# A planned step kernel on one core: a first-user rule, softmax weights of a third unit through DRAM, masked low parts in the weights' place, and another count for later loads

## The chip, the core and the metric

The kernel runs on one core of a Trainium2 chip. The metric is device time in microseconds (us) from one launch, the median of several runs. The engines are called as in the profile: PE (TensorE, matmuls; PEld is its weight load), DVE (VectorE), ACT (ScalarE), POOL (GpSimd) and SP (SyncE), whose queue issues all DMAs of this kernel. Each engine works through its own list in order; what one needs of another it awaits on a semaphore.

## What is computed

One inference step of a decoder with two layers, for 512 rows of a prompt and 8 samples of one row each, with the same weights. Layer A is a gated recurrence of 16 heads (HGRN2), layer B a sliding-window attention of 32 query heads over 4 key heads, window 128, with a sink logit for each head. Around each layer stand RMS norms, a residual and a gated embedding.

```python
def sink_softmax(s, sinks):
    sink = sinks.astype(jnp.float32).reshape(KV_HEADS, Q_PER_KV)[:, :, None, None]
    sink = jnp.broadcast_to(sink, s.shape[:-1] + (1,))
    pr = jax.nn.softmax(jnp.concatenate([s, sink], axis=-1), axis=-1)
    return pr[..., :-1]
...
        mask = in_band & ((cidx >= WINDOW) | (n > 0))
        s = jnp.einsum('bqhgd,bkhd->bhgqk', qn.astype(jnp.float32), kn.astype(jnp.float32)) * ATTN_SCALE
        s = jnp.where(mask, s, -jnp.inf)
        pr = sink_softmax(s, sinks)
        return jnp.einsum('bhgqk,bkhd->bqhgd', pr, vn.astype(jnp.float32))
...
        h = h + rmsnorm(mix, post_norm_g[l])
        h = h + (p[l] @ w_pe[l]) * jax.nn.sigmoid(h @ w_pg[l])
```

## The kernel before

Activations lie transposed, 128 features on the partitions by 520 columns. Every float32 operand of a matmul is split in a high part, rounded to the PE's narrower float32r by a cast on ACT, and a low part, the remainder, mostly from a subtraction on DVE (in the names: wh and wl of weights wr, x or og as pairs). A weight load of 512 KB brings a tile wr; pj are PSUM banks of projections, ph those of everything else.

The program runs through the 16 heads of layer A (their projections, the recurrence, and in groups the output projection out_a), then the boundary (rest of out_a, embedding, the sum of squares acc over x, its reciprocal root rsr, residual, gates, the norm for keys and values), then layer B, then the same kind of boundary again for the end. Layer B has eight units of four query heads. Function unit_proj projects queries and gates of a unit, block makes the softmax for one of four blocks of 128 queries, and out_b projects outputs in groups; out_b(6) of units 2 and 3 stands behind unit 5's projections, out_b(8) of units 4 and 5 behind unit 7's.

In block, W holds the four heads' logits of one block with the sink beside them, in a buffer of tag b3 (blocks 1 and 2) or b2 (blocks 0 and 3), three buffers each. ACT copies the logits there, takes the exponentials and their sum ad, DVE or POOL multiplies by its reciprocal. Then the weights have to be turned so that keys lie on the partitions. For the units in TURN_W that is done by turn_weights: two transposes of 32 x 32 blocks on DVE, one store to a DRAM tile tw and four loads back into W's buffer, then a cast on ACT for the high part and a subtraction for the low one. For all others PE transposes W against an identity (ident) into a PSUM bank, four at a time, and ACT and DVE make both parts from there. In blocks 1 to 3 both parts are also multiplied by a mask (tmask) into ys[0] and ys[1]; up to unit 6 two DMAs then move halves of the masked low part into the empty halves of ys[0].

The order of all instructions is found when the kernel is built, by class Plan. Method enter records an operation with the operations that it depends on: those that wrote or read overlapping regions, and, for every buffered tile that it touches, the tile's maker, the first operation that touched it. Method issue then places one operation after another on the engine that could start it first, by planned costs and delays, and the instructions are held to that order; so all have one line in the profile, L192. Of the operations that an engine could start, choose prefers those whose inputs don't come fresh from a DMA, then by level (MAIN, SIDE, FIRST), then by number. An operation is considered only when its number is less than WINDOW, or for DMAs LOADS, ahead of the lowest one not yet placed (low). An operation entered through either may go to DVE or POOL; POOL takes it where DVE has enough else to do. The point where layer B begins is second.

Of the kernel before, what the change touches and what calls it, by code (L numbers as in the profile page):

```python
# [9 lines left out]
F32 = mybir.dt.float32  # L10
F32R = mybir.dt.float32r
# [10 lines left out]
SEQ = 512  # L22
# [17 lines left out]
PIECE = 4 * P  # L40
SPLITS = 4
TURN_K, TURN_O = range(0, 15), range(1, 15)
TURN_W = (4, 5)
WARM = 17
BEHIND = 4

# [3 lines left out]
MAIN, SIDE, FIRST = 0, 1, 2  # L50
# [44 lines left out]
class Plan:  # L95
# [91 lines left out]
    def enter(self, on, name, a, k):  # L187
        outs = [k["accum_out"]] if "accum_out" in k else []
        outs.append(a[0])
        ins = [x for x in (*a, *k.values()) if isinstance(x, bass.AP)]  # L190
        calls = [getattr(getattr(self.nc, e), name) for e in on]
        op = Op(len(self.ops), self.level, on, [lambda c=c: c(*a, **k) for c in calls],  # L192
                [self.price(e, name, ins, a, k) for e in on], on[0] == "sync")
        if any(x.tensor.name.startswith("tw") for x in ins[1:]):
            op.late = LATE
        self.ops.append(op)
        for x in ins:
            t = x.tensor.name
            r = self.region(x)
            op.deps.update(o for q, o in self.writes.get(t, ()) if self.meet(q, r))  # L200
            self.reads.setdefault(t, []).append((r, op))
            kept = t in self.homes or x.space != bass.MemoryType.DRAM
            if kept and t not in self.left:
                tag, bufs = self.homes.get(t, (t, 1))
                if tag not in self.slots:
                    self.slots[tag] = Slots(tag, bufs)
                self.slots[tag].order.append(t)
                op.news.append((tag, t))
                self.maker[t] = op
            elif kept:  # L210
                op.deps.add(self.maker[t])
            if t not in op.tiles and kept:
                op.tiles.add(t)
                self.left[t] = self.left.get(t, 0) + 1
        for x in outs:
            t = x.tensor.name
            r = self.region(x)
            if on[0] == "tensor":
                r = 0, P, r[2] // 512 * 512, -(-r[3] // 512) * 512
            for book in (self.writes, self.reads):  # L220
                old = book.get(t, [])
                op.deps.update(o for q, o in old if o is not op and self.meet(q, r))
                book[t] = [(q, o) for q, o in old if o is op or not self.within(q, r)]
            self.writes.setdefault(t, []).append((r, op))
        op.deps.discard(op)
        op.load = op.dma and not op.deps
        for d in op.deps:
            d.users.append(op)
        op.open = len(op.deps)
        return op  # L230


    def issue(self):
# [3 lines left out]
        given, pipe, lanes, low, port, slow = set(), 0.0, [0.0] * 8, 0, 0.0, 0.0  # L237
        best = dict.fromkeys(clock)
        stale = set(clock)

        def after(d, e):

            if d.dma:
                return d.end + 0.1
            return d.end + (SAME if d.engine == e else LAT)[d.engine]

        def ready(op, e):
            return max((after(d, e) for d in op.deps), default=0.0)

        def place(op):  # L250
            at = 0.0
# [9 lines left out]
        def choose(e):  # L261
            able = []
            for op, r in wait[e]:
                p = place(op) if op.n < low + (LOADS if op.dma else WINDOW) else None
                if p is not None:
                    held = port if op.cost[op.on.index(e)][1] else 0.0
                    if op.dma and op.load and clock[e] > CALM and pipe > BACKLOG + op.cost[0][0]:
                        held = pipe - BACKLOG - op.cost[0][0]
                    able.append((max(r, p, clock[e], held), op, max(r, p)))
            if not able:  # L270
                return None
            t = min(x[0] for x in able)
            rank = RANK.get(e, OTHER)
            able = [x for x in able if x[0] <= t]
            safe = SAFE if t > CALM and low < self.second else 0.0
            fresh = lambda op: any(d.dma and d.end + safe > t for d in op.deps)
            able.sort(
                key=lambda x: (
                    e == "tensor" and x[2] + HAND > t or e in SHY and fresh(x[1]), rank[x[1].level], x[1].n
                )  # L280
            )
            if e == "gpsimd":
                for x in able:
                    op = x[1]
                    if len(op.on) > 1:

                        free = [
                            o.cost[0][0]
                            for o, r in wait["vector"]
                            if r <= t and not o.cost[0][1] and place(o) is not None  # L290
                        ]
                        if max(clock["vector"] - t, 0.0) * (port <= t) + sum(free) < op.cost[1][0]:
                            continue
                    return x
                return None
            return able[0]
# [6 lines left out]
        while todo:  # L303
# [11 lines left out]
            if op.n == low:  # L315
                while low < len(self.ops) and self.ops[low].engine:
                    low += 1
                stale.update(clock)
            cost, held = op.cost[n]
            if op.dma:  # L320
                t = max(t, lanes[0])
# [69 lines left out]
def in_turn(tiles):  # L391

    for t in tiles[1::2]:
        t.apart = True
    return tiles


def bank_of(ps, h):
# [56 lines left out]
class Step:  # L455
# [871 lines left out]
    def block(self, u, st, n, osb):  # L1327
# [52 lines left out]
                nc.tensor.matmul(po, base[0][:, kvh % 2], w, start=x == 0, stop=x == 1)  # L1380
        else:

            ys = [self.g_(F32R, SEQ) for x in range(2)]
            by = lambda x: x.rearrange("p (i h t) -> p i h t", h=4, t=run)
            mask = spot(self.tmask, 0, (run, P // run), (0, 4), (1, run))
            for x, y in zip((hi, lo), ys):
                nc.either.tensor_tensor(by(y), by(x.bitcast(F32)), mask, op=ALU.mult)
            y, z = (x.bitcast(F32) for x in ys)
            if u < 7:
                nc.sync.dma_start(y[HD:, : 4 * HD], z[:HD, : 4 * HD])  # L1390
                nc.sync.dma_start(y[:HD, 4 * HD :], z[HD:, 4 * HD :])
# [158 lines left out]
    def run(self):  # L1550
# [66 lines left out]
        def done_a(h):  # L1617
# [6 lines left out]

            return f

        for h in range(HEADS):
            tiles += self.proj_a(h, xg if h == 0 else xn, sts[h], done_a(h), R0 if h == 0 else None)
            if h + 1 in groups:
                tiles += out_a(h + 1)  # L1630
        tiles += out_a(17)
        end = out_a(18) + self.embed(0, pe[0], range(E0, KC), kept[0]) + self.embed(1, pe[1], range(E1))

# [47 lines left out]
        for u in range(8):  # L1681
            def done(u=u):
                self.beside(lambda: self.unit_attn(u, us[u]))
                if u % 4 == 3:
                    self.beside(lambda: self.sample_out(u // 4, us[u - 3 : u + 1]), FIRST)

            mine = self.unit_proj(u, qx, us[u], done)
            if u == 7:

                tiles[-2:-2] = mine[:2]  # L1690
                mine = mine[2:]
            tiles += mine
            if u + 1 in ogroups:
                tiles += out_b(u + 1)
        tiles += out_b(9)
        end1 = out_b(10) + self.embed(1, pe[1], range(E1, KC), kept[1])

# [143 lines left out]
```

## Time and profile before

| | |
|---|---|
| Runs, median (lowest to highest) | 1068.3 us (1067.65 to 1070.68, three runs) |
| The profiled execution's own time | 1068.61 us |
| Its span, first to last instruction | 1066.8 us |
| Granted TensorE clock | 0.999 |
| Busy: PE, PEld, DVE, ACT, POOL | 1057.2, 1051.2, 904.7, 681.8, 114.0 us |
| DMA | 178.99 MB, 161 GB/s of HBM over the span |

Busy time is the union of an engine's instructions; matmuls overlap, so a record of 0.28 us doesn't mean that a matmul costs PE as much. The chain of waits follows the work that ended last back in time; the view of waits tells for how long an engine stood still and which engine's result released it.

### The profile page before, as it was taken

Reading aid. Unit: us, or ns where it says so; the run is one execution under the profiler, and the core shown is the slowest. Engines: PE = TensorE matmul, PEld = TensorE weight load, DVE = VectorE, ACT = ScalarE, POOL = GpSimd, SP = SyncE. Lnnn points to the kernel's source line nnn. Section 1 sums busy time; section 2 is a strip of 40 time slices with the busy share of each in tenths; the row PEclk is TensorE's granted clock in tenths of the full one; section 3 lists DMA queues with packets and bytes.
Section 4 is the critical chain, followed back from the end, with each engine's and each line's share of the span. In section 5 each row is a group of like instructions: output and inputs, shape, how many; then the busy total and the mean of one; then the engine's idle time right before and its main releaser. Section 6 shows DMA issues by size and latency. Waiting matters only on the chain.

```text
span 1066.8 us, 23981 instructions
## 1 busy us (share of the span) xinstructions
PE 1057.2 (99%) x8828; PEld 1051.2 (99%) x8828; DVE 904.7 (85%) x1963; ACT 681.8 (64%) x1829; POOL 114.0 (11%) x198
## 2 busy tenths in 40 slices
PE   9999999999999999999999999999999999999998
PEld 8999999999999999999999999999999999999998
DVE  8899788875787958788889999699999998999894
ACT  7877676655767637776636565477667664675542
POOL 1111121101111112111111000000100000002000
PEclk9999999999999999999999999999999999999999
DMA  9556586665646646576663454544433545423432
GB/s 314 183 190 183 143 247 195 191 195 156 213 155 206 193 130 224 177 210 191 190 223 142 159 190 142 170 121 136 124 101 115 164 155 186 154 82 124 156 100 81
DMA packets 147069, 178.99 MB, mean 168 GB/s; under 512 B 76932, under 2 KB 99660, under 8 KB 146952
## 3 DMA queue, kind: packets, MB, share of 16 engines
q1 hardware_dynamic: 146952, 177.46, 52.7%
q8 instruction: 70, 1.15, 0.4%
q14 instruction: 47, 0.39, 0.1%
HBM read 137.04 MB, written 34.86 MB: 161 GB/s over the span
## 4 chain that ended last, share of the span: by engine, by line
PE 91%; ACT 4%; DVE 3%; issue 1%; DMA 0%; POOL 0%; DVEq 0%; POOLq 0%
PE pj L192 71%; PE ph L192 21%; ACT g L192 1%; ACT wh L192 1%; DVE wl L192 1%; DVE x L192 0%; DMA wr<-in_w_pg 0%; ACT tmp L192 0%; ACT sb L192 0%; ACT b L192 0%; DVE acc L192 0%; ACT og L192 0%; DVE xr L192 0%; DVE tmp L192 0%; DVE g L192 0%
## 5 line engine op out<-in xcount | busy, mean ns | idle before, releaser
L192 PE MATMUL pj<-xs,wh 128*128 128x260 f32 (+2 forms) x3264 | 554.7, 285 | 1.6 <-ACT xs L192 1.3
L192 PEld LDWEIGHTS pj<-xs,wh 128*128 128x128 f32 x3264 | 457.7, 189 | 3.2 <-ACT xs L192 2.3
L192 PE MATMUL pj<-xs,wl 128*128 128x260 f32 (+2 forms) x1632 | 340.5, 285 | 0.0
L192 PEld LDWEIGHTS pj<-xs,wl 128*128 128x128 f32 x1632 | 255.1, 188 | 0.2
L192 ACT CAST wh<-wr 128x512 fp32r<-128x512 f32 x287 | 176.2, 619 | 111.1 <-PE pj L192 100.5
L192 DVE TENSOR_TENSOR wl<-wr,wh 128x512 fp32r<-128x512 f32 x275 | 187.6, 685 | 48.6 <-ACT wh L192 47.4
L192 PE MATMUL pj<-og,wh 128*128 128x260 f32 x1056 | 182.4, 285 | 0.3 <-ACT og L192 0.3
L192 PEld LDWEIGHTS pj<-og,wh 128*128 128x128 f32 x1056 | 149.5, 188 | 0.9 <-ACT og L192 0.5
L192 PE MATMUL pj<-og,wl 128*128 128x260 f32 x512 | 106.3, 284 | 0.1
L192 PEld LDWEIGHTS pj<-og,wl 128*128 128x128 f32 x512 | 79.9, 188 | 0.3 <-DVE wl L192 0.3
L192 ACT ACTIVATE sb<-sb,g 128x128 f32<-128x128 f32 x128 | 64.7, 556 | 2.4 <-DVE sb L192 2.4
L192 ACT ACTIVATE sb<-sb,nv 128x128 f32<-128x128 f32 x128 | 63.1, 555 | 0.3
L192 ACT COPY b<-ph 128x256 f32<-128x256 f32 (+1 forms) x80 | 27.8, 350 | 47.0 <-PE ph L192 46.5
L192 ACT ACTIVATE b<-b,an 128x129 f32<-128x129 f32 x128 | 50.6, 398 | 4.5 <-DVE an L192 4.4
L192 ACT ACTIVATE tmp<-pj 128x520 f32<-128x520 f32 (+2 forms) x48 | 24.5, 527 | 43.3 <-PE pj L192 43.2
L192 PE MATMUL ph<-xs,b 128*128 128x256 f32 (+1 forms) x360 | 50.5, 283 | 0.0
L192 DVE COPY_PREDICATED xr<-lmask,ph 128x256 f32<-128x256 int32 x96 | 46.8, 487 | 3.8 <-PE ph L192 3.4
L192 PE MATMUL ph<-xr,b 128*128 128x128 f32 x320 | 49.0, 275 | 0.3 <-ACT b L192 0.3
L192 DVE TENSOR_TENSOR x<-x,pj 128x520 f32<-128x520 f32 (+2 forms) x64 | 39.5, 621 | 10.8 <-PE pj L192 10.2
L192 DVE TENSOR_TENSOR g<-g,b 128x256 f32<-128x256 f32 x96 | 40.5, 422 | 9.3 <-ACT b L192 6.1
L192 DVE TENSOR_TENSOR xr<-xr,b 128x256 f32<-128x256 f32 x96 | 41.0, 427 | 8.6 <-PE ph L192 6.4
L192 PEld LDWEIGHTS ph<-xs,b 128*128 128x128 f32 x360 | 46.3, 188 | 0.1
(222 smaller groups left out, 1737.8 us busy)
## 6 DMA issues: line engine op xcount, KB each, us to landing
wr<-in_w_in_a SPq DMA_DIRECT2D x64, 512.0 KB, 4.5
sb<-sd SPq DMA_DIRECT2D x32, 512.0 KB, 4.5
wr<-in_w_in_b SPq DMA_DIRECT2D x32, 512.0 KB, 4.0
td<-tmp SPq DMA_DIRECT2D x45, 256.0 KB, 3.2
xr<-td SPq DMA_DIRECT2D x180, 64.0 KB, 3.2
sb<-in_state SPq DMA_DIRECT2D x16, 512.0 KB, 5.4
out_st_s<-sb SPq DMA_DIRECT2D x16, 512.0 KB, 3.0
wr<-in_w_out_a SPq DMA_DIRECT2D x16, 512.0 KB, 4.8
```

Of the source, the lines that this page charges most:

```text
L192: op = Op(len(self.ops), self.level, on, [lambda c=c: c(*a, **k) for c in calls], [self.price(e, name, ins, a, k) for e in on], on[0] == " ...
```

## The change

Five edits stand in the diff. TURN_W takes in unit 3. The masked low part ys[1] is written into W's own buffer (home) instead of a g buffer, up to unit 6. A dependency that exists only because another operation was the first to touch the tile becomes soft: it still orders the two, but it counts for nothing in the planned time, nor as fresh from a DMA. From second on, a load of level MAIN is considered by its distance from the next matmul of level MAIN not yet placed, instead of from low. A function weave, which could put the tiles of an output projection between those of the next head or unit, is added; its lists WEAVE_A and WEAVE_B are empty, and then it returns its tiles as they were.

```diff
-TURN_W = (4, 5)
+TURN_W = (3, 4, 5)
+WEAVE_A, WEAVE_B = (), ()
...
+        makers = set()
...
             elif kept:
-                op.deps.add(self.maker[t])
+                makers.add(self.maker[t])
...
         op.deps.discard(op)
+        op.soft = makers - op.deps - {op}
+        op.deps |= op.soft
         op.load = op.dma and not op.deps
...
+        main, front = [op for op in self.ops if op.level == MAIN and "tensor" in op.on], 0
...
-            return max((after(d, e) for d in op.deps), default=0.0)
+            return max((after(d, e) for d in op.deps if d not in op.soft), default=0.0)
...
-                p = place(op) if op.n < low + (LOADS if op.dma else WINDOW) else None
+                first = main[front].n if op.load and op.level == MAIN and front < len(main) and low >= self.second else low
+                p = place(op) if op.n < first + (LOADS if op.dma else WINDOW) else None
...
-            fresh = lambda op: any(d.dma and d.end + safe > t for d in op.deps)
+            fresh = lambda op: any(d.dma and d.end + safe > t for d in op.deps if d not in op.soft)
...
+            while front < len(main) and main[front].engine:
+                front += 1
+                stale.add("sync")
...
+def weave(mine, out):
+
+    n = -(-len(out) // len(mine))
+    return [x for k, t in enumerate(mine) for x in (t, *out[k * n : (k + 1) * n])]
...
-            ys = [self.g_(F32R, SEQ) for x in range(2)]
+            ys = [self.g_(F32R, SEQ), spot(home, 0, (1, SEQ)) if u < 7 else self.g_(F32R, SEQ)]
...
-            y, z = (x.bitcast(F32) for x in ys)
+            y, z = (x.bitcast(F32) if x.dtype == F32R else x for x in ys)
```

What this moves is seen in the order of the instructions. Over the program PE has 16 transposes fewer and DVE eight block transposes more; of the low parts of weights (wl<-wr,wh) POOL has 21 instead of 12, of the multiplications by the reciprocal sum (b<-b,ad) 6 instead of none, and of the mask products 3 instead of 8. Three places in detail.

In unit 3, PE before turns a block's weights (b_2043_2137) between products of the next unit's queries (pj_2217), its logits (ph_2163) and out_b (pj_2280):

```order
L192 MATMUL ph_2163<-xr_1788,g_2094 128x256
L192 MATMUL ph_2163<-xr_1792,g_2094 128x256
L192 MATMUL ph_2144<-ident,b_2043_2137 128x2x64 x4
L192 MATMUL pj_2217<-xs_1725,wh_2209 128x260
L192 MATMUL pj_2280<-og_1890,wh_2212 128x260 x2
```

Now DVE does it, for unit 3's first block (b_2024_2118) in this stretch of its list (g_2187 is a low part of the next unit's queries):

```order
L193 TENSOR_TENSOR wl_2194<-wr_2192,wh_2193 128x512
L193 STREAM_TRANSPOSE tmp_2125<-b_2024_2118 128x2x4x32
L193 SCALAR_TENSOR_TENSOR g_2187<-tmp_2184,g_2186 128x512
L193 STREAM_TRANSPOSE tmp_2125<-b_2024_2118 128x2x4x32
L193 RECIPROCAL ad_2133<-ad_2133 128x4
```

and SP has the stores and loads of unit 3's weights among the loads of weights (wr) and the exchange of queries' halves (qd):

```order
L193 DMA tw_2126<-tmp_2125 128x512
L193 DMA wr_2274<-in_w_out_b 128x1024
L193 DMA g_2186<-qd_2188 64x512
L193 DMA g_2187<-qd_2188 64x512
L193 DMA b_2024_2118<-tw_2126 32x4x128 x2
L193 DMA qd_2199<-g_2197 64x512
L193 DMA b_2024_2118<-tw_2126 32x4x128
L193 DMA qd_2199<-g_2198 64x512
L193 DMA b_2024_2118<-tw_2126 32x4x128
L193 DMA tw_2137<-tmp_2136 128x512
```

So a block's weights now pass from DVE through SP's queue to ACT, and PE's list holds only the products with values.

At the boundary between the layers, PE sums the squares of the first half (ph_1528<-ones,acc_1506) before at this place, behind all of pj_1565, three matmuls of the embedding (pj_1595) and two of ph_1571:

```order
L192 MATMUL pj_1565<-xs_1450,wh_1500 128x264 x2
L192 MATMUL pj_1595<-g_1591,wh_1561 128x260 x2
L192 MATMUL pj_1595<-g_1591,wl_1562 128x260
L192 MATMUL ph_1571<-xs_1379,wh_1504 128x264
L192 MATMUL ph_1571<-xs_1379,wl_1505 128x264
L192 MATMUL ph_1528<-ones,acc_1506 128x1 x2
L192 MATMUL ph_1571<-xs_1380,wh_1504 128x264
```

and now ahead of pj_1565, behind ph_1559:

```order
L193 MATMUL ph_1558<-xs_1450,wh_1495 128x264
L193 MATMUL ph_1559<-xs_1450,wh_1495 128x264
L193 MATMUL ph_1528<-ones,acc_1506 128x1 x2
L193 MATMUL pj_1565<-xs_1379,wh_1500 128x264 x2
L193 MATMUL pj_1565<-xs_1379,wl_1501 128x264 x2
```

It has moved ahead by 17 matmuls. On DVE the additions that it waits for ended before with these rows (wl_1568, a low part of weights, stood on POOL):

```order
L192 TENSOR_TENSOR x_724<-x_724,pj_1556 128x264
L192 TENSOR_TENSOR acc_1506<-acc_1506,tmp_1517 128x256
L192 TENSOR_TENSOR wl_1562<-wr_1560,wh_1561 128x512
L192 TENSOR_TENSOR acc_1506<-acc_1506,tmp_1518 128x256
L192 TENSOR_TENSOR acc_1506<-acc_1506,tmp_1557 128x264
```

and now with these; wl_1568 follows on the same engine, eleven rows behind the last addition (tmp_1518):

```order
L193 TENSOR_TENSOR acc_1506<-acc_1506,tmp_1517 128x256
L193 TENSOR_TENSOR x_719<-x_719,pj_1556 128x264
L193 TENSOR_TENSOR acc_1506<-acc_1506,tmp_1518 128x256
L193 TENSOR_TENSOR x_724<-x_724,pj_1556 128x264
L193 TENSOR_TENSOR wl_1562<-wr_1560,wh_1561 128x512
L193 TENSOR_TENSOR x_728<-x_728,ph_1558 128x264
```

The last addition of the first half (tmp_1518) now stands ahead of x_724 and wl_1562 instead of behind them.

At the start, SP before loads the second part of tmask behind the first weights of layer A:

```order
L192 DMA tmask<-in_tmask 128x64
L192 DMA wr_98<-in_w_pe 128x512
L192 DMA vec<-in_vec 128x88
L192 DMA x_104<-in_xT 128x520
L192 DMA x_105<-in_xT 128x520
L192 DMA x_106<-in_xT 128x520
L192 DMA x_107<-in_xT 128x520
L192 DMA wr_108<-in_w_in_a 128x1024
L192 DMA tmask<-in_tmask 128x64
L192 DMA x_111<-in_xT 128x520
```

and now both parts ahead of them:

```order
L193 DMA tmask<-in_tmask 128x64 x2
L193 DMA wr_98<-in_w_pe 128x512
L193 DMA vec<-in_vec 128x88
L193 DMA x_104<-in_xT 128x520
L193 DMA x_105<-in_xT 128x520
```

One load has moved ahead of seven.

More of the change, by code (lines that the diff above doesn't have):

```diff
@@ L1625, in done_a @@
             return f
+        out = []
         for h in range(HEADS):
-            tiles += self.proj_a(h, xg if h == 0 else xn, sts[h], done_a(h), R0 if h == 0 else None)
-            if h + 1 in groups:
-                tiles += out_a(h + 1)
+            tiles += weave(self.proj_a(h, xg if h == 0 else xn, sts[h], done_a(h), R0 if h == 0 else None), out)
+            out = out_a(h + 1) if h + 1 in groups else []
+            if h + 1 not in WEAVE_A:
+                tiles += out
+                out = []
         tiles += out_a(17)
@@ L1691, in run @@
                 mine = mine[2:]
-            tiles += mine
-            if u + 1 in ogroups:
-                tiles += out_b(u + 1)
+            tiles += weave(mine, out)
+            out = out_b(u + 1) if u + 1 in ogroups else []
+            if u + 1 not in WEAVE_B:
+                tiles += out
+                out = []
         tiles += out_b(9)
```

## The prediction

> **What bounds the kernel now.** I read the page's first and fourth parts, then the windows of 100 us, the chain of waits, and the waits of TensorE by what released it.
>
> ```profile
> span 1066.8 us, 23981 instructions
> ...
> PE 1057.2 (99%) x8828; PEld 1051.2 (99%) x8828; DVE 904.7 (85%) x1963; ACT 681.8 (64%) x1829; POOL 114.0 (11%) x198
> ...
> PE 91%; ACT 4%; DVE 3%; issue 1%; DMA 0%; POOL 0%; DVEq 0%; POOLq 0%
> ```
>
> PE is busy in 99% of the span and carries 91% of the chain that ended last; DVE, the next, is at 85%. The windows (columns: window and its length, then the busy time of PE, PEld, DVE, ACT and POOL) show where this is an average over unlike stages:
>
> ```profile
> 0.00:100.00 100.00, 97.25 (x791) 94.78 (x792) 89.84 (x191) 76.05 (x170) 16.16 (x43) 1.00 0.66 218
> ...
> 700.00:800.00 100.00, 100.00 (x839) 99.65 (x838) 94.82 (x201) 68.56 (x223) 8.29 (x7) 1.00 0.40 122
> 800.00:900.00 100.00, 100.00 (x833) 99.59 (x832) 90.67 (x185) 64.98 (x199) 3.89 (x3) 1.00 0.49 154
> 900.00:1000.00 100.00, 100.00 (x838) 99.58 (x837) 92.50 (x193) 59.86 (x184) 8.34 (x6) 1.00 0.43 143
> ```
>
> From 700 to 1000, where layer B's units run, PE has no gap at all. A busy PE need not be a PE at its pace, so I look for the pace in the chain of waits:
>
> ```profile
> 652.55 33.96 PE pj L192 x283
> ```
>
> 283 matmuls in 33.96 us are 0.120 us each from start to start; that is what a projection matmul costs while nothing holds it up. What PE loses besides is small and has names:
>
> ```profile
> PE pj L192 <- ACT xs L192: 1.3, 2, 0.8
> PE ph L192 <- DVE far L192: 1.1, 1, 1.1
> PE pj L192 <- DVE g L192: 0.9, 2, 0.6
> PE ph L192 <- ACT b L192: 0.5, 2, 0.3
> PE ph L192 <- DVE acc L192: 0.5, 1, 0.5
> PE ph L192 <- POOL rsr L192: 0.4, 1, 0.4
> PE pj L192 <- ACT og L192: 0.3, 1, 0.3
> PE ph L192 <- DVE ad L192: 0.2, 1, 0.2
> ```
>
> That is 5.2 us in all, 1.1 of it the start of the program. So the change can win in two ways only: fewer matmuls, at their pace, or fewer of these waits. And it loses wherever it makes PE wait in a stretch that is full today. No DMA is among the releasers: PE waits for no load.
>
> **The change part by part.**
>
> *Unit 3's weights through DRAM.* Sixteen transposes leave PE (four blocks, four each). What four of them cost stands between the matmuls around them (a block of unit 2; columns: start, time, what, how many):
>
> ```profile
> 788.64 0.40 PE L192 MATMUL pj<-xs,wl 128*128 128x260 f32 x2
> 788.88 0.60 PE L192 MATMUL ph<-ident,b 128*128 128x128 f32 x4
> 789.23 0.73 PE L192 MATMUL pj<-xs,wh 128*128 128x260 f32 x4
> 789.80 0.28 PE L192 MATMUL pj<-xs,wl 128*128 128x260 f32 x1
> ```
>
> From 788.64 to 789.80 are 1.16 us, in which six projection matmuls and four transposes start. Six at 0.12 are 0.72; 0.44 is left for four transposes, 0.11 each. Sixteen: **-1.75 us**, and all of it on the path, since PE is full there. In before the last of unit 3's transposes also wait for the softmax's sum (the 0.2 us of "DVE ad" above); the transposes that wait are gone: **-0.2 us**.
>
> [...]
>
> In their place come eight transposes on DVE and, per block, one store and four loads:
>
> ```profile
> L192 DVE STREAM_TRANSPOSE tmp<-b 128x256 f32<-128x256 f32 x16 | 6.8, 430 | 0.1
> ```
>
> 8 x 0.43 = 3.4 us of DVE. The high part is then cast from SBUF instead of copied out of PSUM, and the low part is subtracted as before: the same count on ACT and DVE. The cover for DVE is what else the order moves. Nine more low parts of weights, six more multiplications by the reciprocal sum go from DVE to POOL, and five mask products come back from POOL:
>
> ```profile
> L192 DVE TENSOR_TENSOR wl<-wr,wh 128x512 fp32r<-128x512 f32 x275 | 187.6, 685 | 48.6 <-ACT wh L192 47.4
> L192 POOL TENSOR_TENSOR wl<-wr,wh 128x512 fp32r<-128x512 f32 x12 | 15.7, 1308 | 215.6 <-ACT wh L192 148.4 <-DMA qd<-g 44.8 <-DVE g L192 22.4
> ```
>
> At 0.685 each DVE gives up 15 and gets 5, -6.9, which with the 3.4 leaves it 3.4 us lighter over the whole program; POOL, at 11%, gets ten more at 1.3 = 13 us. I cost this at **0** on the path, and come back to its other end among the rivals: if POOL's work slows DVE, the cover is gone.
>
> The way through DRAM takes time, and here TensorE may wait. Unit 4's first block shows it (columns as above; the last line is the views' summary of landings for this tile):
>
> ```profile
> 826.89 0.43 DVE L192 STREAM_TRANSPOSE tmp<-b 128x256 f32<-128x256 f32 x1
> 827.38 0.43 SPq L192 DMA_DIRECT2D tw<-tmp  x1
> 831.61 1.76 SPq L192 DMA_DIRECT2D b<-tw  x4
> ...
> 839.33 0.62 ACT L192 CAST g<-b 128x512 fp32r<-128x512 f32 x1
> ...
> DMA to landing us min/median/max: 2.0/3.4/4.8
> ```
>
> The four loads are issued by 833.4, and have landed by 836.8 at the median, by 838.2 at the worst; ACT takes them up at 839.3, so the order leaves 1 to 2.5 us in hand. Eight such trips (units 4 and 5) stand in 800 to 1000, and there PE is full and no DMA is named as a releaser. Unit 3's four trips are written by the same helper and held back by the same allowance. What is late if a trip is late: the cast on ACT, the casts of weights behind it on ACT, then the value matmuls. The nearest rows bound a late trip at 4.8 - 3.4 = 1.4 us of landing beyond the median, four times 5.6. I take **0**, the value of the eight that I see, and keep +5.6 as an end. Unit 3's outputs themselves are in no hurry: out_b's group 8 holds units 4 and 5, and unit 3's partner group 6 stands behind unit 5.
>
> *Masked low parts in the weights' place.* The same multiplications, with another target: 0 of work. The buffer of the weights is held longer, until the move of the masked halves has landed (at most 4.8 us by the row above), and a g buffer is free sooner. What waits if it is late is ACT's copy of a later block's logits. I take 0.
>
> *Loads counted from the next product.* It lets weight loads of layer B start at another time. No PE wait has a DMA as releaser, so there is nothing for it to win: 0; what it can lose is in the wait list too, namely nothing nearer than the start.
>
> *First-user rule.* It deletes no work; it shifts places. Two places matter. At the boundary of the layers:
>
> ```profile
> 573.45 1.46 POOL L192 TENSOR_TENSOR wl<-wr,wh 128x512 fp32r<-128x512 f32 x1 [17.61 <-ACT wh L192]
> 573.69 1.51 DVE L192 TENSOR_TENSOR acc<-acc,tmp 128x256 f32<-128x256 f32 x1
> ...
> 574.47 0.28 PE L192 MATMUL ph<-xs,wl 128*128 128x264 f32 x1
> 575.25 0.52 PEld L192 LDWEIGHTS ph<-ones,acc 128*128 128x128 f32 x4 [0.71 <-DVE acc L192]
> ```
>
> While POOL makes one low part, a sum of squares on DVE takes 1.51 us; its like in the same stage take 0.41 to 0.42. PE starts nothing between 574.47 and 575.25, 0.66 us more than its pace. In the changed order that low part stands on DVE (0.685), which spares it the 1.1 us. PE asks for the sum 17 matmuls (2 us) earlier than before, but the last square and its addition have moved up too: the last addition comes on DVE right behind the first x from pj_1556, 0.8 us for both, and between that product and the sum PE has 12 matmuls, 1.5 us. So I expect this wait gone; but DVE is full in this stage, as the windows of 10 us show, so that what it is spared may be asked for again further on:
>
> ```profile
> 570.00:580.00 10.00, 9.50 (x79) 9.29 (x78) 10.00 (x26) 7.51 (x19) 2.16 (x2) 1.00 0.17 61
> 580.00:590.00 10.00, 9.24 (x76) 8.82 (x75) 10.00 (x23) 6.10 (x17) 1.03 (x1) 1.00 0.61 208
> 590.00:600.00 10.00, 9.73 (x76) 9.10 (x77) 10.00 (x28) 4.62 (x12) 0.00 (x0) 1.00 0.82 296
> 1010.00:1020.00 10.00, 8.87 (x72) 8.37 (x72) 9.81 (x25) 7.45 (x19) 1.83 (x1) 1.00 0.58 197
> ```
>
> PEld falls short by 0.71 + 1.18 + 0.90 = 2.8 us in the 30 us of the boundary, and by 1.6 at its counterpart at the end; those two sums are what the rule could win at most. DVE's balance there is 1.1 spared less 0.685 taken, 0.4; I take **-0.5**, between that and the 0.66, with -2.8 and, for the earlier demand of PE unmet, +0.7 as ends. The counterpart at the end keeps its order but for one matmul less of cover: 0.
>
> The other place is the start, where the queue of SP sends a second load of tmask ahead of the weights, vec and x:
>
> ```profile
> 3.06 0.43 SPq L192 DMA_DIRECT2D tmask<-in_tmask  x1
> ```
>
> One load takes 0.43 of the queue, so all behind it come about 0.5 us later, and what is first asked for shifts PE by no more. Against it stand the waits of the first 100 us in the list (far, b and og, 1.9 in all), among whose neighbours the order has been changed: I take 0, with -1 and +0.5 as ends.
>
> **Sum**: -1.75 - 0.2 - 0.5 = -2.45. The profiled execution took 1068.61 us, 1.8 beyond its span; 1068.61 - 2.45 = 1066.2. It lies 0.3 above the median of the runs, 1068.3, from which the same sum gives 1065.9. I say **1066.0**.
>
> **The rivals.** A measurement of this kernel can tell 0.3%, 3.2 us, from no change: faster is below 1065.1, slower above 1071.5.
>
> First, *the new order clears the boundary altogether*, not only its first wait: -1.95 for unit 3, -2.8 at the boundary, and half of the 1.6 at its counterpart, together -5.55: 1063.0. For it speaks that squares and additions are interleaved earlier; against it that DVE stays at 10.00 of 10 in all three windows, and that the later waits of the stage are for xs, which the sum of squares only begins. Chance 0.29.
>
> Second, *nothing is left of it*: small waits of 0.2 to 0.6 us, the size of those in the list, arise at five or so of the many places that the order has shifted, and take the 2.45 back: 1068.3. For it: PE is full, so every slip shows. Against: the order is planned by the same costs that left no gap from 600 to 1000. Chance 0.15.
>
> Third, on the other side, *POOL holds DVE up in layer B*. The row at 573.69 gives the price: 1.51 - 0.42 = 1.1 us of DVE for one operation beside POOL. In the new order twelve operations of 1.3 us (six low parts, five products with the reciprocal, one mask) stand on POOL between unit 0's third block and unit 3's second, about 100 us. If each costs DVE 1.1, that is 13 us, against the 5.2 that DVE has free in 700 to 800; 8 us are over, and from the point at which DVE is behind by more than the order's lead PE pays them: 1068.6 + 8 - 2.45 = 1074. Against it: twenty such operations (twelve low parts, eight masks) stand on POOL before, and PE shows no gap there; the wait list names the one at the boundary alone. Chance 0.08.
>
> [...]
>
> **How the numbers follow.** The forecast, 1066.0 give or take 1.2, has 0.48; by its lower edge some 0.04 of it lies under 1065.1. Faster: 0.29 + 0.04 = 0.33. Same: 0.44 + 0.15 = 0.59. Slower: 0.08. The range takes in the first rival at 1063.0 with 0.2 for the start, and above it the second with the start's and a late trip's 1.4 us, 1068.3 + 1.9 = 1070.2; it leaves out the third and the far tail of the first: 1062.8 to 1070.2.
>
> **What would show it.** Right: PE has 16 matmuls on ident,b fewer; the windows from 700 to 1000 stay at 100.00; the waits for acc at the boundary and for ad are gone; unit 3's casts of weights wait for no DMA; the end of the units comes 2 to 2.5 us earlier. The first rival: PEld in 570 to 600 above 29 of 30. The second: new waits in the list, each under 1 us, in windows that are full now. The third: DVE operations of 1.3 us and more beside POOL's between 690 and 800, and a PE wait on DVE there. It would be wrong altogether if a trip of unit 3 holds ACT, seen as ACT waiting for b from tw and PE below 100 near 790 to 820, or if the start shifts by more than 1 us.

## The result and the profile after

The changed kernel took **1072.0 us** (median of 14 runs, 1070.2 to 1074.7), the kernel before 1068.4 (14 runs beside them). The ratio is 1.0033, 95% interval 1.0025 to 1.0041: slower by 3.6 us, outside the predicted range and on the other side. The profile at hand is that of the fastest run, 1070.23 us; two more were taken later (1072.07 and 1073.58).

```profile
span 1068.4 us, 24010 instructions
...
PE 1056.9 (99%) x8812; PEld 1049.7 (98%) x8812; DVE 906.9 (85%) x1969; ACT 681.3 (64%) x1829; POOL 124.1 (12%) x200
```

PE has the 16 matmuls fewer and is still busy for 99%: the averages hide the loss. Among PE's waits, those of the list before for acc, ad and rsr are gone. New are the first line (products with values, which wait for a low part from DVE), another such product that waits for ACT, and logits that wait for a DMA:

```profile
PE ph L193 <- DVE g L193: 1.9, 2, 1.1
PE pj L193 <- ACT xs L193: 1.2, 4, 0.4
...
PE ph L193 <- ACT g L193: 0.5, 1, 0.5
PE ph L193 <- DMA g<-qd: 0.4, 1, 0.4
```

The windows of 100 us (columns as in the prediction) say where. The boundary is better than before (98.47), the units are worse: the stretch that had no gap has one of 2 us.

```profile
500.00:600.00 100.00, 99.42 (x836) 98.80 (x835) 90.28 (x205) 56.02 (x149) 10.89 (x16) 1.00 0.64 204
...
700.00:800.00 100.00, 98.02 (x814) 96.79 (x813) 95.01 (x199) 66.89 (x222) 14.90 (x12) 1.00 0.38 118
```

A window's length less its PEld busy time, called the shortfall from here on, is the time in which PE loads no weights; it is finer than PE's own busy time, but a slower pace doesn't show in it. By stage, in us, for two profiles of before and three of after (with the time of each profiled run), and for the run pool_cut below:

| Stage | before 1068.61 | before 1068.24 | after 1070.23 | after 1072.07 | after 1073.58 | pool_cut 1069.27 |
|---|---|---|---|---|---|---|
| 0 to 110, start | 5.2 | 5.7 | 5.5 | 4.6 | 5.4 | 4.6 |
| 110 to 530, layer A | 0.1 | 0.0 | 0.6 | 1.0 | 2.9 | 2.2 |
| 530 to 630, boundary | 2.8 | 1.8 | 1.2 | 1.2 | 1.2 | 1.2 |
| 630 to 1000, layer B | 1.6 | 2.0 | 5.8 | 5.5 | 6.4 | 2.3 |
| from 1000, end | 5.9 | 6.0 | 5.5 | 5.5 | 5.5 | 5.5 |

Layer B loses some 4 us in every profile of after (3.5 to 4.8), layer A 0.5 to 2.9 more; the boundary wins 0.6 to 1.6 and the end some 0.4. The two values of 4.6 at the start are no gain: in those two profiles PE ran at half pace for a while (last section) and had started 864 and 867 matmuls by 110 us, against 875 in the first profile of after.

What happens at the two largest waits of layer B is in the timeline (start, time, engine, what):

```profile
697.12 1.31 POOL L193 TENSOR_TENSOR g<-g,tmask 128x512 fp32r<-128x512 f32 x1 [42.20 <-ACT g L193]
697.17 1.81 DVE L193 TENSOR_TENSOR tmp<-tmp,tmp 128x520 f32<-128x520 f32 x1
...
698.90 0.68 DVE L193 TENSOR_TENSOR g<-ph,g 128x512 fp32r<-128x512 f32 x1
...
699.63 0.39 PE L193 MATMUL ph<-g,x 128*128 128x256 f32 x1 [0.84 <-DVE g L193]
...
760.43 2.38 DVE L193 TENSOR_TENSOR og<-ao,og 128x512 fp32r<-128x512 f32 x2
760.67 1.59 POOL L193 TENSOR_TENSOR wl<-wr,wh 128x512 fp32r<-128x512 f32 x1 [4.12 <-issue]
762.74 0.68 DVE L193 TENSOR_TENSOR g<-ph,g 128x512 fp32r<-128x512 f32 x1
...
763.47 0.50 PE L193 MATMUL ph<-g,x 128*128 128x512 f32 x1 [1.08 <-DVE g L193]
```

POOL starts an operation that reads SBUF; DVE's operation with two SBUF inputs that stands beside it takes 1.81 us where its like takes 0.69 (at 706.52), and two of them take 2.38 (1.28 in the run pool_cut below); the low part that PE waits for (g<-ph,g) is next in DVE's list and comes a microsecond late. That is the third rival's mechanism. The experiments ask whether it is the cause, and what else is.

### The profile page after: what moved, and what is told of

Read it like the earlier page. It is cut to its first block, busy times and chain, and to the rows that moved or that the text cites. A ratio compares the mean times of both kernels' runs of the same rounds, so it can differ in the third digit from the quotient of the medians.

```text
span 1068.4 us, 24010 instructions
## 1 busy us (share of the span) xinstructions
PE 1056.9 (99%) x8812; PEld 1049.7 (98%) x8812; DVE 906.9 (85%) x1969; ACT 681.3 (64%) x1829; POOL 124.1 (12%) x200
## 4 chain that ended last, share of the span: by engine, by line
PE 91%; ACT 3%; DVE 3%; DMA 2%; SPq 1%; issue 0%; DVEq 0%; ACTq 0%
PE pj L193 70%; PE ph L193 21%; DVE tmp L193 1%; SPq L193 1%; DMA td<-tmp 1%; ACT g L193 1%; ACT wh L193 1%; ACT b L193 0%; ACT og L193 0%; DMA g<-qd 0%; ACT tmp L193 0%; DMA x<-in_xT 0%; DVE ao L193 0%; DVE b L193 0%; ACT sb L193 0%
## 5 line engine op out<-in xcount | busy, mean ns | idle before, releaser
L193 DVE TENSOR_TENSOR wl<-wr,wh 128x512 fp32r<-128x512 f32 x266 | 182.7, 689 | 58.2 <-ACT wh L193 57.5
L193 POOL TENSOR_TENSOR wl<-wr,wh 128x512 fp32r<-128x512 f32 x21 | 29.0, 1380 | 246.0 <-ACT wh L193 239.8
L193 ACT COPY b<-g 128x256 f32<-128x256 f32 (+1 forms) x112 | 40.5, 376 | 16.2 <-DVE g L193 10.6
```

## The experiments

Theories: A, POOL holds DVE up in layer B; B, unit 3's way through DRAM; C, the first-user rule plans too early; D (formed on the way), DVE has no room in layer B. Each ratio is to the kernel before, run beside it.

**One edit at a time.** The kernel before with one edit:

```diff
-TURN_W = (4, 5)
+TURN_W = (3, 4, 5)
```

> Only unit 3's softmax weights go through DRAM; the other three edits are undone. POOL has 10 low parts of weights, 6 masks and 1 product with the reciprocal sum. Theory A (POOL holds DVE up in layer B, and PE waits for the operation held up): no more of POOL's work than before stands in layer B, so the 16 transposes show as forecast: 1066.5, PE full from 690 to 800. Theory B (unit 3's way through DRAM is what costs, by DVE's 3.4 us more and by late trips): 1070 or more, with PE waits near 780 to 830. Theory C (the first-user rule plans operations for earlier than they can start): as A, 1066.5.

Measured: 1076.7 us, ratio 1.0079 (1.0067 to 1.0092).

```diff
+        op.soft = makers - op.deps - {op}
+        op.deps |= op.soft
```

> Only the first-user rule. POOL has 16 low parts, 6 masks and 2 products; the mask g_1863 and the product b_1771 of unit 0 stand on POOL as in the changed kernel. Theory A: the boundary gains about 1.8 us as in the changed kernel, and the waits of unit 0 (1.0 and 0.6 us near 700 and 707) are there because a DVE operation beside POOL takes 0.7 to 1.1 us longer; about 1068. Theory B: none of the loss is here, only the boundary's gain: 1066.5. Theory C: all of the loss is here, 1072 to 1074 (the 16 transposes are not saved), with waits that have no POOL operation beside them.

Measured: 1072.1, ratio 1.0036 (1.0023 to 1.0049).

```diff
-            ys = [self.g_(F32R, SEQ) for x in range(2)]
+            ys = [self.g_(F32R, SEQ), spot(home, 0, (1, SEQ)) if u < 7 else self.g_(F32R, SEQ)]
```

> Only the masked low parts in the weights' buffer. POOL has 9 low parts, 5 masks, 3 products. Theory A: fewer operations on POOL than before in layer B, so no loss from there: 1068.4 plus or minus 1. Theories B and C: 1068.4. If the buffers come free too late, ACT's copies of logits wait and PE has gaps in 690 to 1000: above 1070.

Measured: 1073.2, ratio 1.0043 (1.0030 to 1.0055).

```diff
+                first = main[front].n if op.load and op.level == MAIN and front < len(main) and low >= self.second else low
```

> Only the count of later loads from the next product. POOL has 15 low parts, 7 masks, 1 product, more low parts in layer B than before (10 after the boundary begins, instead of 7). Theory A: a loss wherever one of them stands beside a DVE operation with two SBUF inputs that PE waits for; 1068.4 to 1070. Theories B and C: 1068.4.

Measured: 1070.1, ratio 1.0018 (1.0009 to 1.0028).

Every edit loses by itself, even the ones that add no work: 8.4, 3.8, 4.9 and 1.9 us, 19 together, and all of them at once lose 3.6. So the losses don't belong to the edits as such: each brings another order of layer B, and layer B's shortfall (630 to 1000; 1.6 and 2.0 before) is 9.3, 4.7, 5.8 and 3.2. The expectations of 1066.5 to 1068.4 failed in the same way: an order that nobody had seen run was taken to be as tight as the one that had. Theory B has its number in turn_alone (1070 or more), but not its place: between 700 and 870 PE waits once, for 0.2 us, and the large waits stand at 886 to 893, where the trips are unit 5's. One of the trips holds ACT for 0.95 us, at 819.63, and PE doesn't wait there. Theory C has its number in firstuser_alone (1072), but it expected waits with no POOL operation beside them: those near 700 and 708 stand behind DVE operations of 1.82 and 1.44 us beside POOL's, as in the changed kernel.

**POOL's work taken out, the order kept.** The changed kernel in its own order, but POOL's optional operations of layer B do 4 columns only, so that POOL hardly reads:

```diff
+            if e == "gpsimd" and len(op.on) > 1 and low >= self.second:
+                name, a, k = op.raw
+                few = lambda x: x[(slice(None), *[slice(0, 1)] * (len(x.shape) - 2), slice(0, 4))]
+                if a[0].tensor.name != a[1].tensor.name:
+                    self.tc.keep_in_program_order(self.nc.gpsimd.memset(a[0].bitcast(F32), 0.0))
+                self.tc.keep_in_program_order(getattr(self.nc.gpsimd, name)(*[few(x) for x in a], **k))
+            else:
+                self.tc.keep_in_program_order(op.calls[n]())
```

> The changed kernel in its own order on every engine, but POOL's 17 optional operations of layer B leave their work out: each is done for 4 columns only (the outputs that are not made in place are filled by a write-only memset first), so the results of those blocks are not the reference's. Same waits, same places, hardly a read by POOL. Theory A (DVE operations beside POOL's are held up, and PE waits for them): the waits at 699.8, 707.6 and 763.5 us (1.1 + 0.5 + 1.1) go, and 1072.0 falls by 2.5 to 4: 1068 to 1069.5. Theory C (the new order is too tight in layer B by itself): 1072 plus or minus 1, the same three waits.

Measured: 1069.1, ratio 1.0003 (0.9995 to 1.0012): 2.95 us less than the changed kernel. At the first of the two places the same rows now read:

```profile
699.79 0.68 DVE L193 TENSOR_TENSOR tmp<-tmp,tmp 128x520 f32<-128x520 f32 x1
...
699.81 0.73 POOL L324 TENSOR_TENSOR g<-g,tmask 128x4 fp32r<-128x4 f32 x1 [36.77 <-ACT g L193]
...
700.06 0.52 PE L193 MATMUL ph<-g,x 128*128 128x512 f32 x2
700.39 0.67 DVE L193 TENSOR_TENSOR g<-ph,g 128x512 fp32r<-128x512 f32 x1
```

and at the second:

```profile
760.34 1.28 DVE L193 TENSOR_TENSOR og<-ao,og 128x512 fp32r<-128x512 f32 x2
...
762.99 0.39 PE L193 MATMUL ph<-g,x 128*128 128x512 f32 x1
```

The same two operations start at nearly the same moment, DVE's takes 0.68, and PE waits for nothing, at neither place. Layer B's shortfall falls from 5.8 to 2.3. The edit also makes POOL's own results come sooner, but in the first profile of after no wait of PE in the list names POOL. On the page, DVE's busy time of 906.9 us in after has become 901.9:

```profile
PE 1057.7 (99%) x8812; PEld 1051.3 (99%) x8812; DVE 901.9 (85%) x1969; ACT 680.9 (64%) x1829; POOL 112.3 (11%) x211
```

The control does the same to the kernel before:

> Control: the kernel before in its own order, with the 14 optional operations of POOL in layer B left out in the same way as in the run pool_cut (4 columns, a write-only memset ahead), so the results of those blocks are not the reference's. Theory A: no DVE operation held up there is one that PE waits for, so nothing to win: 1068.4 plus or minus 0.5. If leaving work out on POOL is a gain whatever the order, the 2.95 us of pool_cut say nothing about the change: 1066.

Measured: 1068.6, ratio 1.0000 (0.9991 to 1.0008). There POOL's work in layer B costs nothing that can be measured. So the 3 us belong to the places at which the new order puts it.

**More work for POOL, the old order kept.**

```diff
+            if e == "vector" and len(op.on) > 1 and low >= self.second and op.raw[1][0].tensor.name.startswith("wl"):
+                self.seen = getattr(self, "seen", 0) + 1
+                if self.seen in range(12, 48, 3):
+                    _, a, k = op.raw
+                    self.tc.keep_in_program_order(self.nc.gpsimd.tensor_tensor(a[1], *a[1:], **k))
```

> The kernel before, every other engine in its own order, with 12 more operations on POOL between unit 0 and unit 4: behind each third low part that DVE makes, POOL subtracts once more into the raw weights, which nobody reads again. Theory A: each holds up a DVE operation with two SBUF inputs by up to 1.1 us, 5 to 13 us of DVE in a stretch with 5 us free in 100; PE pays a third to a half: 1071 to 1074, with PE waits for DVE between 690 and 860. If POOL does not matter to DVE: 1068.4 plus or minus 0.5, PE full as before.

Measured: 1074.3, ratio 1.0056 (1.0044 to 1.0069). In 690 to 870 (PE, PEld, DVE, ACT, POOL), first this kernel:

```profile
690.00:870.00 180.00, 176.59 (x1455) 173.76 (x1454) 170.78 (x339) 122.45 (x388) 29.06 (x21) 1.00 0.40 118
```

and the kernel before:

```profile
690.00:870.00 180.00, 179.79 (x1502) 178.94 (x1501) 167.15 (x348) 124.77 (x396) 10.89 (x9) 1.00 0.42 127
```

18 us more on POOL made DVE's time 3.6 us longer, with fewer instructions in the window, and cost PEld 5.2. Nobody reads what these operations make, so it isn't POOL's results that come late. The time is a little above theory A's range; it makes half a microsecond of PE for each operation here (5.9 us for 12), which is no price for every place: in the control 14 operations cost nothing.

**Are the other losses of the same kind?** Unit 3's weights alone and the masks alone, with POOL's work taken out in the same way:

> Unit 3's weights through DRAM alone (1076.7), with POOL's optional operations of layer B left out in that way. Theory A: the 8.4 us began with a DVE operation of 1.79 us beside POOL at 872.7; without it 1066.5 to 1069. Theory D (DVE has no room left: it is busy without a gap from 868 to 893 there, with the transposes as the last straw): 1073 or more, the same waits at 887 to 893.

Measured: 1075.7, ratio 1.0069 (1.0057 to 1.0081): 1 us less than turn_alone, with intervals that overlap, and a shortfall in layer B of 9.4 instead of 9.3. So POOL is not the cause here. The number is theory D's, and so are the waits, which stay: in turn_alone PE waits 0.5, 2.2, 1.2 and 0.7 us within 6 us, for ACT, DVE, ACT and DVE, and DVE works without a gap from 869 to 890, unit 5's transposes among the rest. But theory D as a lack of room is not shown. From 868 to 889 DVE is as full in the kernel before, where PE has no gap,

```profile
868.00:889.00 21.00, 21.00 (x178) 21.00 (x177) 20.05 (x44) 13.23 (x46) 1.29 (x1) 1.00 0.49 170
```

as in this run:

```profile
868.00:889.00 21.00, 18.31 (x148) 17.60 (x146) 20.00 (x42) 12.01 (x45) 0.87 (x2) 0.97 0.34 105
```

It is then likely the order in which DVE comes to the results that PE needs; which place in it costs, no run shows. After the waits PE pays once more, as the windows of turn_alone show (the column behind POOL's is the granted clock):

```profile
886.00:890.00 4.00, 1.32 (x6) 0.54 (x4) 3.82 (x8) 1.01 (x3) 0.00 (x0) 1.00 0.77 254
890.00:894.00 4.00, 1.93 (x7) 1.37 (x6) 3.25 (x7) 2.39 (x6) 0.00 (x0) 0.73 1.02 345
894.00:898.00 4.00, 4.00 (x19) 3.89 (x19) 1.97 (x4) 1.72 (x3) 0.00 (x0) 0.50 0.91 261
898.00:902.00 4.00, 4.00 (x33) 4.00 (x32) 2.88 (x4) 1.31 (x3) 1.44 (x1) 0.92 0.93 288
```

> Masked low parts in the weights' buffer alone (1073.2), with POOL's optional operations of layer B left out. Theory A: 1068.4 to 1070. If instead a late buffer or move is what costs there: 1072 to 1074.

Measured: 1070.4, ratio 1.0018 (1.0009 to 1.0027): 2.7 of 4.9 us are POOL's. A wait for xs of 1.5 us at the end stays; its cause stays open.

**Taking POOL's help away instead.** The boundary's rule (below), unit 3's weights through DRAM, and no optional operation for POOL in layer B:

```diff
-                        if max(clock["vector"] - t, 0.0) * (port <= t) + sum(free) < op.cost[1][0]:
+                        if max(clock["vector"] - t, 0.0) * (port <= t) + sum(free) < op.cost[1][0] + (9.0 if low >= self.second else 0.0):
```

> The same, and unit 3's weights through DRAM, and a planner that gives POOL no optional operation in layer B (those 14 or so go to DVE). Theory A says that no DVE operation is held up there, so PE waits less; but DVE gets 9.6 us for those and 3.4 us for the transposes, with 22 us free in 700 to 1000. If that fits: 1067.0 - 1.75 = 1065.3. If DVE becomes the bound in places, as it was for 16 us in the run with unit 3's weights alone: 1068 to 1072.

Measured: 1082.3, ratio 1.0133 (1.0113 to 1.0153), the slowest of all. DVE does everything now, at 106.18 us busy of 110 from 690 to 800:

```profile
690.00:800.00 110.00, 109.41 (x911) 108.51 (x911) 106.18 (x222) 78.86 (x257) 0.20 (x1) 1.00 0.38 110
...
870.00:900.00 30.00, 24.63 (x171) 22.96 (x171) 25.88 (x53) 15.71 (x53) 0.00 (x0) 0.84 0.48 161
```

So POOL without work in layer B is no remedy by itself. That DVE needs POOL's help is likely but not shown: the run makes a new order too, and at 888 to 895 it has turn_alone's row of waits again (0.6, 2.8, 1.2 and 0.6 us), which POOL didn't cause there. Letting the planner keep its `port` held for 0.6 us longer behind each POOL operation of layer B doesn't help either:

```diff
-                    port = op.end
+                    port = op.end + (0.6 if e == "gpsimd" and low >= self.second else 0.0)
```

> The changed kernel with a planner that takes the port to be held 0.6 us longer behind each POOL operation in layer B, so that DVE operations with two SBUF inputs are planned further from them; the order of layer B is new, POOL has 20 low parts, 8 masks, 3 products. Theory A: fewer are held up; 1068 to 1070. Theory D: POOL's help on DVE comes later, DVE is short: 1072 or more.

Measured: 1075.5, ratio 1.0062 (1.0050 to 1.0074); that too is a new order of layer B, with a shortfall of 7.0 there and 3.5 in layer A.

**Which part of the first-user rule does what.** The rule for a range of operation numbers alone, on the kernel before:

```diff
+        op.soft = makers - op.deps - {op} if not hasattr(self, 'second') else set()
```

> The first-user rule only for operations entered before layer B begins; the other three edits undone. From the first unit to the second boundary every engine has the order of before. Theory A and C alike: the boundary's gain is kept (stalls of 3.3 us there fell to 1.4 in the changed kernel), the first half gives back 0.7, and layer B's waits are not there: 1067.3. If the loss came from the first half through what it leaves behind (late loads, buffers), layer B would lose again: 1070 or more.

Measured: 1069.6, ratio 1.0014 (1.0004 to 1.0025), slower, not faster. Layer B, in its old order, has no loss:

```profile
630.00:1000.00 370.00, 369.78 (x3088) 368.43 (x3088) 338.01 (x718) 233.53 (x716) 23.42 (x19) 1.00 0.47 141
```

Layer A's shortfall is 1.2 in this profile; the boundary's is 2.0, so the gain that was expected there isn't made. With the range from 6000 to second:

```diff
+        op.soft = makers - op.deps - {op} if 6000 <= op.n < 7717 else set()
```

> The kernel before with the first-user rule for the operations around the boundary only (numbers 6000 to the start of layer B). Layer A up to some 500 us, layer B's units and the end have the order of before. The boundary's stalls fall from 3.3 us to between 1.4 and 2.2, as in the changed kernel and in the one with the rule for all of layer A: 1067.0 (1066.6 to 1067.5). If DVE, full there, gives nothing back: 1068.4.

Measured: 1069.1, ratio 1.0004 (0.9995 to 1.0013): no difference, and a shortfall of 2.3 at the boundary. With numbers below 300:

```diff
+        op.soft = makers - op.deps - {op} if op.n < 300 else set()
```

> The kernel before with the first-user rule for the first 300 operations only (start, masks, embedding); everything later in its old order. In the changed kernel the first real matmul starts at 5.49 us instead of 5.24, and in one profile of two PE then runs at half pace until 10.2 us (11 matmuls in 2 us instead of 19), 1.4 us more. If the start is one part of the loss: some runs at 1068.7, others at 1070, median 1069 to 1070. If it is chance and has nothing to do with the order: 1068.4 plus or minus 0.3.

Measured: 1069.2, ratio 1.0005 (0.9996 to 1.0014): no difference. The changed kernel without the rule for those 300:

```diff
-        op.soft = makers - op.deps - {op}
+        op.soft = makers - op.deps - {op} if op.n >= 300 else set()
```

> The changed kernel with the start of before (the first-user rule from operation 300 on), everything else in its order. If the start is one part of the loss: 1072.0 falls by 0.3 to 1.4, to about 1071, and the runs lie closer together. Theory A alone: 1072, as layer B is the same.

Measured: 1073.0, ratio 1.0042 (1.0028 to 1.0055). The start is no part of the loss that can be measured.

**More profiles**, of the changed kernel twice and of the kernel before once, with no edit.

> The changed kernel once more for another profile, since its runs reach from 1070.2 to 1074.7 and the profile at hand is of the fastest. All theories: 1070 to 1075. Theory A: what a longer run loses more stands in layer B behind DVE operations beside POOL's; theory C: anywhere behind late DMAs or DVE.

> The changed kernel a third time. Theory A: the waits of layer B for DVE operations beside POOL's at about 699.8 and 763.5 are there again, some 4 us of stall more than before between 630 and 1000; what makes runs differ is the start (full or half pace until 10 us) and single stalls in layer A.

> The kernel before once more, for a second profile. In two kernels with its order of layer A a stall of 1.4 to 3.3 us stood near 150 us that the first profile does not have. If it is chance: there or not, with PE full from 690 to 1000 in either case. If it belonged to the changed starts and boundaries: not there, 1067.5 to 1069.

Measured: 1072.07, 1073.58 and 1068.24 (one run each); the table above has them. Layer B's loss is in all three profiles of after. The second lacks the wait at the first of the two places shown above: there the two operations started at 698.83 and 698.86, and POOL's was the one held up (1.88 us, DVE's 0.70). In layer A one wait of 1 us stands in the slowest of the three only. SP's queue and PE's product of transposed tiles in before:

```profile
208.82 1.92 SPq L192 DMA_DIRECT2D xr<-td  x3
210.79 0.62 SPq L192 DMA_DIRECT2D sb<-sd  x1
...
216.55 1.13 PE L192 MATMUL ph<-xr,xr 128*128 128x128 f32 x8
```

and in the third profile of after:

```profile
209.50 0.93 SPq L193 DMA_DIRECT2D sb<-sd  x2
211.40 2.73 SPq L193 DMA_DIRECT2D xr<-td  x4
...
219.46 1.13 PE L193 MATMUL ph<-xr,xr 128*128 128x128 f32 x8 [0.97 <-DMA xr<-td]
```

Both sb loads now stand ahead of xr's, and from the end of xr's issues to the product are 5.3 us with a wait of 1 us in them, where before had 5.8 with none. In the first profile of after the same product starts 4.5 us behind the issues without a wait. So the new order leaves over a microsecond less for the landing, and the landing is sometimes later than that: a wait of this product for xr stands in four of the eight profiles with the rule in layer A (0.2, 0.8, 1.0 and 2.1 us) and in none of the twelve without. This fits the loss of firstuser_layer_a, whose own profile lacks the wait; it wasn't tried by moving that load alone. Other stalls there come and go in kernels with the order of before as well (3.2 us of shortfall in start_only's profile, 1.5 in boundary_only's).

## Why the prediction was wrong

- **POOL, "I cost this at 0 on the path"**: the step that failed. It is 3 us (pool_cut 2.95, with its control at 0). The working says that DVE becomes 3.4 us lighter and that "if POOL's work slows DVE, the cover is gone". By the page DVE became 2.2 us heavier (904.7 to 906.9), and with POOL's work of layer B taken out 2.8 lighter (901.9): the balance was nearly right, and POOL took it back. From "twenty such operations stand on POOL before, and PE shows no gap there" I concluded that POOL is harmless. The control shows what that sentence was worth: it holds for the order of before and no other. In the new order two of the held-up operations (at 697.17 and 760.43) stand right ahead of a low part that PE asks for, and PE waits 0.8 and 1.1 us; a third, 1.43 us at 702.11 and 0.68 in pool_cut, comes before a wait of 0.5 us at 707.42 that pool_cut doesn't have.
- **The third rival** described the place and the mechanism, and had a chance of 0.08. Its size, 8 us, was too large: it charged PE for all that DVE loses beyond its free time, and in the rows shown PE pays only where a held-up operation stands ahead of a result that PE waits for.
- **Against the second rival, "the order is planned by the same costs that left no gap from 600 to 1000"**: the same error in general form. Five other orders from that planner, with one small edit each or a port held for longer, have shortfalls of 3.2 to 9.3 us in layer B. That before has 1.6 is a property of that order, not of the planner.
- **Layer A**: not in the sum at all. The first-user rule was weighed at two places, and it has moved loads in all of layer A; the shortfall there is 0.5 to 2.9 us larger. Part of this may be chance, as start_only's 3.2 in the old order of layer A shows.
- **Sixteen transposes, -1.75**: about right at best. PEld's busy time on the page was 1051.2 and 1051.1 in the two profiles of before, 1049.7 and 1050.4 in the first and third of after, 0.7 to 1.5 us less; in the second, with the start at half pace, it is 1052.2. The wait for ad is gone, as said.
- **Boundary, -0.5**: right in size, by luck. 1.8 fell to 1.2 against the second profile of before, but the 0.66 us for acc, on which I rested it, stands in the first profile alone, and 1 us of the first rival's 2.8 was chance.
- **Trips through DRAM, 0**: right in after. No wait of ACT in 780 to 840 names tw.
- **Masked low parts and loads, 0 each**: alone they lost 4.9 and 1.9 us, in orders of their own, so neither number is a price in the changed kernel. There no wait of PE names a load of weights. (That no DMA is among PE's releasers in before holds for its first profile; the second has a wait of 0.3 us for a move g<-g.)
- **Start, 0 with +0.5 as an end**: right in size. The first real product starts 0.25 us later.

In the fastest run, 1070.23 us, layer B alone is as large as the miss: the sum from the profiled execution of before was 1066.2, some 4 us less, and layer B's shortfall is 4.2 us larger. The two slower profiles add a loss in layer A or at the start.

At 697.17 DVE's operation has two SBUF inputs, POOL's beside it reads SBUF, and 1.12 us are lost (1.81 against 0.69); in pool_cut, where POOL reads 4 columns only, the same operation takes 0.68. What it is in the two that makes one hold the other up, no run here shows.

What stays open: the last part of the difference between pool_cut (1069.1) and the forecast (1066.0), 3.1 us. Its profile has 2.2 us of shortfall in layer A and a slow start (below; 12 matmuls in 8 to 10 us instead of 19, and 8 matmuls fewer by 110 us than the first profile of after, an estimated 1.0 us at 0.12 each). Together they are about as large as the gap, but this is one profile, and that either is the change's doing isn't shown. No version that I ran beats the kernel before.

## What to carry to other kernels

When one engine is full and an order keeps it so, the absence of waits is a property of that order, and a change that makes a planner lay it out anew must be charged for new waits even where it saves work: here some 1 us of work was saved and some 4 us of waits came in layer B alone. To know whether an engine off the path costs anything, take its work out with the order kept, and do the same to the kernel before as a control. That an engine is busy without a gap where PE waits is not yet a cause: look at the same stretch where PE doesn't wait. A wait that stands in one profile may be chance; take a second profile before a forecast rests on it.

## What was not expected of the hardware

PE's pace fell to about half at times. In turn_alone PE had started only 13 matmuls in 8 us when the granted clock went to 0.73 and then 0.50, and 19 matmuls instead of 33 started in 4 us. At 0.12 us each the 14 that are missing are an estimated 1.7 us, on top of waits of 4.6. At the start a pace of about half stands in two of the twenty profiles, the second of after and pool_cut, without showing in that column. In the second profile of after, from 8 to 10 us (granted clock 1.00):

```profile
8.00:10.00 2.00, 2.00 (x11) 2.00 (x11) 1.44 (x3) 1.21 (x2) 0.00 (x0) 1.00 1.04 336
```

and in the first:

```profile
8.00:10.00 2.00, 2.00 (x19) 2.00 (x18) 2.00 (x8) 1.17 (x4) 0.00 (x0) 1.00 1.00 288
```

11 matmuls against 19 in the same 2 us, both "full" by busy time, both at a granted clock of 1.00: here the count of instructions tells a pace that neither the busy time nor the granted clock does. What brings the half pace on no run here shows. In turn_alone it stands behind waits of 4.6 us, with a granted clock of 0.50. The two slow starts are among eight profiles with the changed start, and the twelve with the old start have none, too few to tell chance from the change.
